# Moving a weight-staging loop's transfers from SyncE's queue to ScalarE's, with fetches two steps ahead

## The chip, the core and the metric

The kernel runs on one core of one Trainium2 chip. The metric is the device time of one execution in microseconds (us). Before the change the median of three runs is 2617.11 us (2611.94 to 2621.6). The profiled execution, from which all durations below come, took 2616.91 us.

## What is computed

One inference step of a decoder trunk with two layers on 1024 prompt tokens and 8 x 8 sample tokens, 1088 in all, with 1024 channels, in float32. Every layer adds three things to the running state h:

```python
def swiglu_ffn(x, w_gu, w_down):
    g, u = jnp.split(x @ w_gu, 2, axis=-1)
    return (jax.nn.silu(g) * u) @ w_down
...
        h = h + mix
        h = h + swiglu_ffn(rms_norm(h, g_ffn[i]), ffn_w_gu[i], ffn_w_down[i])
        gate = jax.nn.sigmoid(rms_norm(h, g_ple[i]) @ ple_w_gate[i])
        h = h + gate * (p[i] @ ple_w_proj[i])
```

The mixer `mix` is a short gated convolution in layer 0 and a Conformer convolution module in layer 1. A final norm follows. The states of the convolutions are outputs too.

## The kernel before

**Products.** Every weight matrix is cut into units of 128 x 1024 float32 (512 KB); the array `wall` holds them in the order of first use. A float32 product is made from three float32r products: `block` multiplies the weight's rounded part `whi` with both parts of the activation and the weight's remainder `wlo` with the first. A unit has 8 blocks of 128 x 128. With all 1088 tokens (three chunks of 288, 512 and 288 columns) a block is 9 matmuls.

**Preparing a unit.** `fetch_to` (L175) fetches a raw unit from SyncE's queue into one of two buffers `wraw`. `prep_to` rounds it on ScalarE (`whi`) and subtracts on GpSimd (`wlo` = `wraw` - `whi`). There are three buffers each of `whi` and `wlo`, so that a unit is prepared when TensorE has finished the unit three earlier. Right after the subtraction's place in the program the next raw unit is fetched; that fetch waits until GpSimd has read the old one.

**Staging.** From the end of layer 0's mixer on, most units are used twice, since the 1088 tokens are then split into two groups (GA, GB). While layer 0's feed-forward runs (`ffn(GJ, 0, ...)`, all 1088 tokens at once), `stage` computes the remainders of the 110 later units ahead of time and stores them in DRAM (`dlo`); `prep_to` then fetches a staged remainder (L221) where it would else subtract. `item` calls `stage` after every block, and it acts when TensorE's modelled time has moved on by STAGE_EVERY = 6.3. One step does three things:

- it stores the remainder of the step before (`dlo` <- `slo`, L242, SyncE's queue);
- it fetches a raw unit (`sraw` <- `wall`, L247, SyncE's queue; two buffers);
- it rounds the unit fetched in the step before (`shi`, ScalarE, one buffer) and subtracts (`slo` = `sraw` - `shi`, GpSimd, three buffers).

What is left when the layer's last product has been emitted is staged at once, in a loop in `run`.

**The feed-forward layer.** 22 tiles of 128 hidden channels. For each, `up` makes two items of 8 blocks, one unit each: the gate, then the other half. Behind the gate's item come VectorE (`t` = ps x r), ScalarE (silu, `t` <- `t`) and GpSimd (`t` x r); behind the second item come VectorE (`t` = ps x `t`), ScalarE (`act`, the rounded part) and VectorE (`act`'s remainder). After each group of hidden tiles (FFN_SPLIT = [3, 2, 2, 3, 3, 3, 3, 3]) `hidden` emits one more up tile and then eight down items of 3 or 2 blocks, each with a VectorE add into h (`add_h`: `h` <- `ps`, `h`), which frees the item's PSUM tile. In this stretch there are two PSUM tiles `ps`.

**Order.** Nothing is scheduled by a tool: every engine and every queue carries out its instructions in the order in which the program emits them. A helper (`Paced`, L121) stands between, so that all compute instructions have the line L121 in the profile; the tiles' names tell them apart. DMAs have their own lines.

Of the kernel before, what the change touches and what calls it, by code (L numbers as in the profile page):

```python
# [13 lines left out]
F32 = mybir.dt.float32  # L14
F32R = mybir.dt.float32r
AF = mybir.ActivationFunctionType
ALU = mybir.AluOpType
PSUM = bass.MemoryType.PSUM

P = 128  # L20
D = 1024
KD = D // P
# [115 lines left out]
class Net:  # L138
# [92 lines left out]
    def stage(self):  # L231


        nc = self.nc
        if nc.tensor.at < self.stage_at or self.pst is None:
            return
        self.stage_at = max(self.stage_at + self.STAGE_EVERY, nc.tensor.at - 2 * self.STAGE_EVERY)
        done, self.staging = self.staging, None
        if done is not None:
            u, lo = done  # L240
            self.staged[u] = self.pd.tile([P, KD * P], F32, name=f"dlo{u}")
            nc.sync.dma_start(self.staged[u], lo.bitcast(F32))  # L242
        ready = list(self.stage_raw)
        if self.to_stage:
            u = self.to_stage.popleft()
            raw = self.pst.tile([P, KD * P], F32, name="sraw", tag="sraw", bufs=2)
            nc.sync.dma_start(raw, self.wall[u])  # L247
            self.stage_raw.append((u, raw))
        if ready:
            u, raw = self.stage_raw.popleft()  # L250
            hi, lo = (
                self.pst.tile([P, KD * P], F32R, name=n, tag=n, bufs=b) for n, b in (("shi", 1), ("slo", 3)))
            nc.scalar.wait(nc.tensor)
            nc.scalar.activation(hi, raw, AF.Copy)
            nc.gpsimd.wait(nc.scalar)
            nc.gpsimd.tensor_tensor(lo, raw, hi.bitcast(F32), ALU.subtract)
            self.staging = u, lo


    def block(self, g, ps, blk, x, first, last):  # L260
# [619 lines left out]
    def run(self):  # L880
# [44 lines left out]
        for j in range(KD):  # L925
# [3 lines left out]
            if j == 5:  # L929
                self.prep_to(self.RING)  # L930
            if j >= self.LAG:
                self.norm_stat(GJ, j - self.LAG, nc.vector)
        for j in range(KD - self.LAG, KD):
            self.norm_stat(GJ, j, nc.vector)
# [122 lines left out]
    T_BUFS = 5  # L1057
    COST_B = 1.6
    STAGE_EVERY = 6.3
    LAG = 3  # L1060
    WARM = 12
    RB_GATE = 4
# [119 lines left out]
```

## Time and profile before

| | |
|---|---|
| median of three runs | 2617.11 us |
| profiled execution | 2616.91 us, of it the span 2615.1 us |
| TensorE busy | 2538.8 us (97%) |
| weight loads (PEld) busy | 2300.0 us (88%) |
| VectorE, ScalarE, GpSimd busy | 1091.9 (42%), 911.2 (35%), 992.9 us (38%) |
| mean granted TensorE clock | 0.986 |
| DMA queue of SyncE (q1) | 424.53 MB, 47.8% of 16 engines' span |
| DMA queue of ScalarE (q10) | 2.23 MB, 0.3% |

PE is TensorE, PEld its weight loads, DVE VectorE, ACT ScalarE, POOL GpSimd, SPq and ACTq the issuing of DMAs on SyncE and ScalarE. "Idle before, releaser" names what ended an engine's idle time. A DMA's issue is short; "to landing" is the time from the issue until the data are there. DMA-issuing instructions do not count as busy time of their engine.

### The profile page before, as it was taken

The numbers are of one execution on the slowest core, as the hardware profiler recorded it, in microseconds if no ns is written. First come the engines' busy times: TensorE is split into PE (matmuls) and PEld (weight loads), VectorE is DVE, ScalarE is ACT, GpSimd is POOL, SyncE is SP. The second block draws the span as 40 slices with busy tenths as digits, with TensorE's granted clock in tenths as the row PEclk, the third lists the DMA queues.
The fourth block names the chain that finished last, engine by engine and source line by source line (L and its number), as shares of the span: only waits on it lengthen the run. The fifth ranks groups of instructions, "written<-read, shape, count | busy, mean of one in ns | idle before, by whom it ended". The sixth has DMA issues, their size and how long they took to land.

```text
span 2615.1 us, 36216 instructions
## 1 busy us (share of the span) xinstructions
PE 2538.8 (97%) x15062; PEld 2300.0 (88%) x15062; DVE 1091.9 (42%) x1546; ACT 911.2 (35%) x1106; POOL 992.9 (38%) x552
## 2 busy tenths in 40 slices
PE   9999999899899999989999999999999999999997
PEld 8999998798798898989879997888887899999997
DVE  5222242222212212123487776788875442222235
ACT  5111133232222222223554545444335532222235
POOL 3323245665565665655233333333332210000012
PEclk9999999999999999999999999999999999999999
DMA  3111113555555555554555465555555575444445
GB/s 129 58 50 43 42 49 134 179 186 185 185 176 195 182 175 189 180 195 143 174 195 191 173 175 185 186 187 189 187 192 180 198 258 199 168 165 166 162 163 196
DMA packets 143236, 429.07 MB, mean 164 GB/s; under 512 B 33888, under 2 KB 37344, under 8 KB 143072
## 3 DMA queue, kind: packets, MB, share of 16 engines
q1 hardware_dynamic: 141920, 424.53, 47.8%
q8 instruction: 118, 1.93, 0.3%
q10 hardware_dynamic: 1152, 2.23, 0.3%
q14 instruction: 46, 0.38, 0.0%
HBM read 358.94 MB, written 67.76 MB: 163 GB/s over the span
## 4 chain that ended last, share of the span: by engine, by line
PE 53%; DVE 2%; ACT 1%; DMA 1%; issue 0%; POOL 0%; DVEq 0%; SPq 0%; ACTq 0%
PE ps L121 53%; DVE t L121 0%; DMA wlo<-dlo 0%; DVE h L121 0%; DVE acc L121 0%; DMA dlo<-slo 0%; DVE act L121 0%; DVE hna L121 0%; DVE nt L121 0%; ACT ua L121 0%; ACT act L121 0%; ACT cact L121 0%; DVE nv L121 0%; POOL slo L121 0%; ACT whi L121 0%
## 5 line engine op out<-in xcount | busy, mean ns | idle before, releaser
L121 PE MATMUL ps<-hn,whi 128*128 128x288 f32 (+3 forms) x6528 | 1324.9, 325 | 2.6 <-ACT whi L121 2.4
L121 PEld LDWEIGHTS ps<-hn,whi 128*128 128x128 f32 x6528 | 1014.2, 189 | 88.3 <-ACT whi L121 2.6
L121 PE MATMUL ps<-hn,wlo 128*128 128x288 f32 (+3 forms) x3264 | 796.3, 325 | 3.2 <-DMA wlo<-dlo 3.2
L121 PE MATMUL ps<-act,whi 128*128 128x288 f32 (+1 forms) x2496 | 526.0, 336 | 48.3 <-DVE h L121 44.0
L121 PEld LDWEIGHTS ps<-hn,wlo 128*128 128x128 f32 x3264 | 525.3, 189 | 45.3 <-DMA wlo<-dlo 3.4
L121 PEld LDWEIGHTS ps<-act,whi 128*128 128x128 f32 x2496 | 398.0, 193 | 90.8 <-DVE h L121 46.4
L121 ACT ACTIVATE whi<-wraw 128x1024 fp32r<-128x1024 f32 (+1 forms) x326 | 339.1, 1042 | 275.6 <-PE ps L121 238.3
L121 POOL TENSOR_TENSOR slo<-sraw,shi 128x1024 fp32r<-128x1024 f32 x110 | 263.7, 2398 | 306.0 <-ACT shi L121 256.4
L121 POOL TENSOR_TENSOR t<-t,r 128x1088 f32<-128x1088 f32 (+2 forms) x74 | 136.3, 1842 | 544.3 <-ACT t L121 499.2
L121 POOL TENSOR_TENSOR wlo<-wraw,whi 128x1024 fp32r<-128x1024 f32 (+1 forms) x98 | 258.7, 2641 | 159.4 <-ACT whi L121 143.3
L121 DVE TENSOR_TENSOR h<-ps,h 128x1088 f32<-128x1088 f32 (+2 forms) x216 | 205.0, 952 | 249.8 <-PE ps L121 249.5
L121 PE MATMUL ps<-act,wlo 128*128 128x288 f32 (+1 forms) x1248 | 309.1, 334 | 0.0
L121 ACT ACTIVATE shi<-sraw 128x1024 fp32r<-128x1024 f32 x110 | 116.6, 1060 | 520.1 <-DMA sraw<-wall 487.9
L121 DVE TENSOR_TENSOR t<-ps,t 128x1088 f32<-128x1088 f32 (+2 forms) x89 | 80.8, 908 | 425.4 <-PE ps L121 330.7
L121 DVE TENSOR_TENSOR t<-ps,r 128x512 f32<-128x512 f32 (+4 forms) x138 | 107.4, 780 | 309.8 <-PE ps L121 309.0
L121 POOL TENSOR_TENSOR sqacc<-sqacc,sq 128x512 f32<-128x512 f32 (+4 forms) x76 | 117.9, 1552 | 275.1 <-ACT sq L121 274.7
L121 PEld LDWEIGHTS ps<-act,wlo 128*128 128x128 f32 x1248 | 203.1, 192 | 19.1
L121 POOL TENSOR_TENSOR prod<-prod 128x512 f32<-128x512 f32 x96 | 124.3, 1303 | 182.8 <-ACT prod L121 182.7
L121 DVE TENSOR_TENSOR act<-t,act 128x1088 fp32r<-128x1088 f32 (+2 forms) x74 | 98.8, 1336 | 169.3 <-ACT act L121 169.3
L121 ACT ACTIVATE t<-t 128x512 f32<-128x512 f32 (+4 forms) x106 | 75.8, 716 | 244.9 <-DVE t L121 244.8
L121 ACT ACTIVATE act<-t 128x1088 fp32r<-128x1088 f32 (+2 forms) x74 | 62.1, 839 | 250.0 <-DVE t L121 250.0
L121 DVE SCALAR_TENSOR_TENSOR acc<-ub,vecs_sb,acc 128x512 f32<-128x512 f32 x184 | 137.7, 750 | 4.0 <-ACT acc L121 4.0
(123 smaller groups left out, 1684.5 us busy)
## 6 DMA issues: line engine op xcount, KB each, us to landing
wraw<-wall SPq DMA_DIRECT2D x322, 512.0 KB, 3.9
wlo<-dlo SPq DMA_DIRECT2D x226, 512.0 KB, 3.4
sraw<-wall SPq DMA_DIRECT2D x110, 512.0 KB, 6.7
dlo<-slo SPq DMA_DIRECT2D x110, 512.0 KB, 5.4
h<-xT SPq DMA_DIRECT2D x8, 544.0 KB, 6.9
pp<-t SPq DMA_DIRECT2D x8, 288.0 KB, 2.4
ub<-pp SPq DMA_DIRECT2D x8, 288.0 KB, 4.8
pp<-t SPq DMA_DIRECT2D x8, 256.0 KB, 2.7
```

What stands on the lines that cost most here:

```text
L121: return f(out, *args, **kw)
```

## The change

Staging's stores and raw fetches are issued from ScalarE. The fetch runs two steps ahead of its use (STAGE_AHEAD), with five buffers `sraw`. GpSimd writes the remainder over the raw unit, so that `slo` is gone; `dlo` is stored from `sraw`. In one step the order is now: store of the step before, rounding, subtraction, fetch. The memory is the same (six tiles of 128 x 1024 in both). The planner's model of ScalarE's time is brought up to TensorE's at each step; the order on TensorE and VectorE is the same as before.

```diff
         done, self.staging = self.staging, None
+        nc.scalar.wait(nc.tensor)
         if done is not None:
             u, lo = done
             self.staged[u] = self.pd.tile([P, KD * P], F32, name=f"dlo{u}")
-            nc.sync.dma_start(self.staged[u], lo.bitcast(F32))
-        ready = list(self.stage_raw)
+            nc.scalar.dma_start(self.staged[u], lo)
+        ready = len(self.stage_raw) == self.STAGE_AHEAD or not self.to_stage
+        if ready and self.stage_raw:
+            u, raw = self.stage_raw.popleft()
+            hi = self.pst.tile([P, KD * P], F32R, name="shi", tag="shi", bufs=1)
+            nc.scalar.activation(hi, raw, AF.Copy)
+            nc.gpsimd.wait(nc.scalar)
+            nc.gpsimd.tensor_tensor(raw.bitcast(F32R), raw, hi.bitcast(F32), ALU.subtract)
+            self.staging = u, raw
         if self.to_stage:
             u = self.to_stage.popleft()
-            raw = self.pst.tile([P, KD * P], F32, name="sraw", tag="sraw", bufs=2)
-            nc.sync.dma_start(raw, self.wall[u])
+            raw = self.pst.tile([P, KD * P], F32, name="sraw", tag="sraw", bufs=self.STAGE_AHEAD + 3)
+            nc.scalar.dma_start(raw, self.wall[u])
             self.stage_raw.append((u, raw))
-        if ready:
-            u, raw = self.stage_raw.popleft()
-            hi, lo = (
-                self.pst.tile([P, KD * P], F32R, name=n, tag=n, bufs=b) for n, b in (("shi", 1), ("slo", 3)))
-            nc.scalar.wait(nc.tensor)
-            nc.scalar.activation(hi, raw, AF.Copy)
-            nc.gpsimd.wait(nc.scalar)
-            nc.gpsimd.tensor_tensor(lo, raw, hi.bitcast(F32), ALU.subtract)
-            self.staging = u, lo
...
     STAGE_EVERY = 6.3
+    STAGE_AHEAD = 2
```

ScalarE's queue early in the layer, from one up tile's silu (`t<-t`) over its second unit to its `act` and into the next unit. Before:

```order
L121 ACTIVATE t<-t 128x1088
L121 ACTIVATE whi<-wraw 128x1024
L121 ACTIVATE shi<-sraw 128x1024 x2
L121 ACTIVATE act<-t 128x1088
L121 ACTIVATE whi<-wraw 128x1024
```

The same place after the change:

```order
L121 ACTIVATE t<-t 128x1088
L121 ACTIVATE whi<-wraw 128x1024
L121 DMA dlo_3355<-sraw 128x1024
L121 ACTIVATE shi<-sraw 128x1024
L121 DMA sraw<-wall 128x1024
L121 DMA dlo_3398<-sraw 128x1024
L121 ACTIVATE shi<-sraw 128x1024
L121 DMA sraw<-wall 128x1024
L121 ACTIVATE act<-t 128x1088
L121 ACTIVATE whi<-wraw 128x1024
```

Each rounding now stands between a store and a fetch; two of each lie ahead of `act`. SyncE's queue at about the same place (`dlo` with a number is one staged unit in DRAM). Before:

```order
L175 DMA wraw<-wall 128x1024
L242 DMA dlo_3258<-slo 128x1024
L247 DMA sraw<-wall 128x1024
L242 DMA dlo_3302<-slo 128x1024
L247 DMA sraw<-wall 128x1024
L175 DMA wraw<-wall 128x1024
```

After, from the mixer's last state outputs to the first remainders fetched back:

```order
L476 DMA sa_p<-u_2458 128x2
L477 DMA sa_s<-u_2458 1024x1x2
L175 DMA wraw<-wall 128x1024 x68
L221 DMA wlo<-dlo_3183 128x1024
L175 DMA wraw<-wall 128x1024
L221 DMA wlo<-dlo_3250 128x1024
L175 DMA wraw<-wall 128x1024
```

The staged fetches and stores that stood between weight fetches are gone from this queue: 68 weight fetches follow one another. At the layer's start ScalarE has, before, `whi`, `shi`, `whi`, `sh` (the norm's sum), and after the change `whi`, `whi`, `sh`, `shi`, since the first rounding comes one step later.

## Prediction

> **What bounds the kernel now.** I read the page's totals first, then what TensorE waited for, then the stretch in which staging runs. The page's first lines and the list of TensorE's waits (us in total, times, longest):
>
> ```profile
> span 2615.1 us, 36216 instructions
> PE 2538.8 (97%) x15062; PEld 2300.0 (88%) x15062; DVE 1091.9 (42%) x1546; ACT 911.2 (35%) x1106; POOL 992.9 (38%) x552
> ...
> PE ps L121 <- DVE h L121: 44.0, 7, 10.3
> ...
> PE st L121 <- DVE sl L121: 1.3, 1, 1.3
> ```
>
> TensorE is busy for 97% of the span, so only its holes and its slow stretches can be won. 44.0 us of some 76 us of holes are seven waits for a VectorE add into h. Next, busy time by stretches (us: PE busy with its matmuls, the other engines, granted clock, DMA share, GB/s): a clean stretch, a staging stretch, and the whole first feed-forward layer. Behind them comes its costliest waiting group:
>
> ```profile
> 100.00:200.00 100.00, 100.00 (x605) 91.12 (x604) 23.87 (x24) 14.98 (x16) 28.99 (x16) 1.00 0.15 46
> 600.00:700.00 100.00, 87.85 (x506) 79.78 (x507) 27.48 (x21) 25.07 (x25) 56.98 (x23) 0.93 0.51 174
> 393.60:1253.40 859.80, 810.79 (x4761) 735.08 (x4760) 214.20 (x153) 248.35 (x247) 508.75 (x204) 0.97 0.52 176
> ```
> ```profile
> L121 PE MATMUL ps<-act,whi 128*128 128x288 f32 (+1 forms) x1056 | 217.8, 344 | 47.2 <-DVE h L121 44.0 <-DVE t L121 2.7 <-DVE act L121 0.5
> ```
>
> The clean stretch runs 605 matmuls in 100 us, 165.3 ns each. At that pace the layer's 4761 need 787.0 us; it takes 859.8. So 72.8 us are lost in it. All seven waits for h lie in it, with 2.7 for t, 0.5 for act and 1.3 for the norm's sum: 48.5 us stand still, and the other 24 us are matmuls at a lower clock behind those stops (0.93 granted in 600 to 700).
>
> What makes h late? The timeline around one of the seven, engine by engine (start, duration, what, [idle before <- releaser]):
>
> ```profile
> 1009.20 0.33 SPq L175 DMA_DIRECT2D wraw<-wall  x1
> 1009.58 0.42 SPq L242 DMA_DIRECT2D dlo<-slo  x1
> 1010.05 0.43 SPq L247 DMA_DIRECT2D sraw<-wall  x1
> ```
> ```profile
> 1016.56 1.06 ACT L121 ACTIVATE shi<-sraw 128x1024 fp32r<-128x1024 f32 x1 [11.15 <-DMA sraw<-wall]
> 1017.52 1.09 ACT L121 ACTIVATE act<-t 128x1088 fp32r<-128x1088 f32 x1
> ```
> ```profile
> 1007.53 1.29 DVE L121 TENSOR_TENSOR t<-ps,t 128x1088 f32<-128x1088 f32 x1 [10.70 <-PE ps L121]
> 1018.65 2.54 DVE L121 TENSOR_TENSOR act<-t,act 128x1088 fp32r<-128x1088 f32 x1 [9.82 <-ACT act L121]
> 1021.11 2.48 DVE L121 TENSOR_TENSOR h<-ps,h 128x1088 f32<-128x1088 f32 x2
> ```
> ```profile
> 1006.75 2.42 POOL L121 TENSOR_TENSOR wlo<-wraw,whi 128x1024 fp32r<-128x1024 f32 x1
> ```
> ```profile
> 1022.44 1.94 PE L121 MATMUL ps<-act,whi 128*128 128x288 f32 x5 [6.14 <-DVE h L121]
> ```
>
> VectorE has t at 1008.8. ScalarE could make act then, but shi stands ahead of it in its queue and waits for a staged tile until 1016.56. So act comes 8.7 us late, h behind it, and TensorE, with both PSUM tiles full, stops for 6.14. The tile was asked for only at 1010.05: SyncE was held at the weight fetch (L175) until GpSimd finished wlo at 1009.17, and the staged fetch queues behind that. The totals for 400 to 1215 say that this is the rule (ScalarE, then SyncE):
>
> ```profile
> ACT shi L121 <- DMA sraw<-wall: 487.9, 63, 12.5
> ACT shi L121 <- POOL slo L121: 32.0, 39, 1.6
> ```
> ```profile
> SPq L175 <- POOL wlo L121: 626.3, 63, 16.4
> ```
>
> It is a ring of latencies: shi, GpSimd's subtractions, SyncE, a landing, the next shi.
>
> **The change part by part.** Its durations (min/median/max ns, first and last start us; landings in us) for sraw, for slo, and for the eight DMAs that ScalarE issues today:
>
> ```profile
> L247 SPq DMA_DIRECT2D sraw<-wall x110: 328/430/778, 403.1 to 1204.8; - x110
> L121 ACT ACTIVATE shi<-sraw x110: 1041/1061/1067, 407.6 to 1210.6; 128x1024 fp32r<-128x1024 f32 x110
> DMA to landing us min/median/max: 4.5/6.7/9.0
> ```
> ```profile
> L121 POOL TENSOR_TENSOR slo<-sraw,shi x110: 2343/2402/2441, 408.7 to 1212.3; 128x1024 fp32r<-128x1024 f32 x110
> L242 SPq DMA_DIRECT2D dlo<-slo x110: 326/423/1481, 414.9 to 1214.7; - x110
> DMA to landing us min/median/max: 3.6/5.4/8.4
> ```
> ```profile
> L121 ACTq DMA_DIRECT2D praw<-pT x8: 334/358/454, 1260.0 to 1468.6; - x8
> ```
>
> *Fetch two steps ahead.* The 110 fetches spread over 801.7 us, 7.36 us a step; without the layer's loss of 72.8 a step is (801.7 - 72.8)/109 = 6.7 us. A tile asked for two steps ahead has 13.4 us to land, against 9.0 at worst. ScalarE's 487.9 us at shi go, and with them the lateness of act. SyncE keeps only weight fetches in this stretch: 626.3 us of waiting stay there, with nothing staged behind.
>
> *Store on ScalarE.* It waits for GpSimd's subtraction of the step before. Queued behind it: shi, the next fetch, act, whi. But shi waits for the same subtraction today, since its one buffer is read by it (the 32.0 us row); the wait moves one place ahead and costs nothing new. The fetch gains a wait: its buffer, one of five, is free once the store issued two steps earlier has landed, 8.4 at worst against 13.4. Nothing there either.
>
> *220 issues on ScalarE.* One costs 0.33 (praw's minimum) to 1.48 us (the worst store on SyncE); I take 0.43, sraw's median, some 95 us in all, which leaves ScalarE well under half used. What matters is the place ahead of act, so I lay out the last up unit, with these rows besides:
>
> ```profile
> L121 DVE TENSOR_TENSOR t<-ps,r x22: 1278/1292/1293, 420.6 to 1204.9; 128x1088 f32<-128x1088 f32 x22
> L121 ACT ACTIVATE t<-t x22: 1091/1113/1117, 424.4 to 1206.3; 128x1088 f32<-128x1088 f32 x22
> L121 POOL TENSOR_TENSOR t<-t,r x22: 2498/2540/2572, 425.6 to 1207.5; 128x1088 f32<-128x1088 f32 x22
> ```
> ```profile
> L121 POOL TENSOR_TENSOR wlo<-wraw,whi x64: 2361/2408/3467, 400.3 to 1220.4; 128x1024 fp32r<-128x1024 f32 x64
> L121 ACT ACTIVATE whi<-wraw x63: 1039/1043/1066, 408.5 to 1219.3; 128x1024 fp32r<-128x1024 f32 x63
> ```
> ```profile
> L121 DVE TENSOR_TENSOR act<-t,act x22: 1293/2600/3381, 430.6 to 1219.4; 128x1088 fp32r<-128x1088 f32 x22
> ```
>
> Let TensorE end that unit at 0; it began at 72 x 165.3 ns before, at -11.9. VectorE's t: -10.6. Silu: -9.5. whi, store, shi, fetch: -6.5. GpSimd from -9.5: t, wlo, first subtraction: -2.1. Then the second store, shi and fetch on ScalarE: -0.2. VectorE's t of the second half comes at 1.3, so act starts on time with 1.5 us in hand. At 1.48 per issue the last fetch ends near 1.9, 0.6 late.
>
> From there: t 1.3, act 2.4, VectorE's act 3.7 to 5.0 (1.29 free, 2.60 beside GpSimd), h 5.0 to 6.3. TensorE needs that PSUM tile after two down items: two times three blocks of 9 matmuls, 8.9 us, or in the two groups with two blocks, 6.0 us. Slack 2.6 in the former; up to 0.3 missing in the latter. I keep 0.5 at each of those two, the 0.5 for act at the layer's end, and 1.5 for small stops: 3 us.
>
> *Remainder over the raw tile.* The same 110 subtractions; only the destination is new. No row shows one in place at this size, but t<-t,r is in place: 2.54 us for 1088 columns, 2.33 ns a column, against 2.34 for slo. The bound is the slowed 3.47 of wlo's row: +1.07 each, covered by GpSimd's idle time (508.75 busy of 859.8).
>
> *Order at the start.* With the first shi behind sh, the norm's sum no longer waits for a staged tile: the 1.3 goes with the rest.
>
> Sum, against the profiled execution's own time of 2616.9 (span 2615.1 and 1.8 around it; the median of the three timed runs is 2617.1, the same): 2616.9 - 72.8 + 3 = 2547. The clean pace is uncertain by one matmul in 605, 1.3 us on 787; I say 2548.
>
> How much of the loss comes back with the stops hangs on the clock. Behind the 2.7 us stop at 501 (start, duration) six matmuls took 2.02 us, and 1.17 a little later:
>
> ```profile
> 503.36 2.02 PE L121 MATMUL ps<-act,whi 128*128 128x288 f32 x6
> ...
> 506.08 1.17 PE L121 MATMUL ps<-act,whi 128*128 128x288 f32 x6
> ```
>
> So even this stop, short beside the others, has slow matmuls behind it, and I let all 24 us go. The Trainium skill ("TensorE: Matmul & The Clock Gate", "HAM oscillation") has half rate only behind idle gaps over about 3.4 us, one window of that length each. By that rule five or six of the stops would cost 1.7 us each, the gain would be 48.5 + 10 - 3, and the time, as an estimate from that page, 2561. The trace disagrees: it misses 24 us where the rule has 10.
>
> **The rivals.** *ScalarE or GpSimd is late next (2556 to 2595).* Issues at 1.48 make act 0.6 late, felt only at the two short groups; subtractions at 3.47 make the last up unit's GpSimd work 2.5 + 3 x 3.5 = 13 us against 11.9. Then some of the seven stops stay at a few us each, each with its slow matmuls (24 lost beside 48.5: half as much again). Half of the loss kept is 2616.9 - 36 = 2581. For it: GpSimd is the busiest helper here (56.98 of 100). Against: it now idles, waiting for shi.
>
> *No change (2604 to 2630).* If staged tiles asked for by ScalarE landed later than 13.4 us, shi would wait as now. Against: the DMA share is 0.52 over the layer, and the tile above landed 6.5 us after its issue; the delay was ahead of the issue. The Trainium skill ("DMA: Bandwidth & Descriptors", "Issuing engines are not separate DMA queues") speaks for this rival: issuing from several engines saves only the sequencer's issue time. The trace shows what that leaves out here: 626.3 us of waiting ahead of the issues.
>
> *Slower (2640 and up).* The fetch now holds ScalarE until the store of two steps earlier has landed. With landing L, two steps take L + 2 us (issues and shi). Against 13.4 this begins at L = 11.4; at L = 12.7 the 55 pairs take 55 x 14.7 = 809 against 737, as much as today's loss, and at 14 they take 880, so 2616.9 - 72.8 + 143 = 2687. It needs landings 1.5 times the worst seen, from two queues colliding. Against: the rows show 8.4 at worst, with weight fetch, store and staged fetch issued within a microsecond as above; the change spreads them.
>
> **How the numbers follow.** Forecast 0.76, late helpers 0.12, no change 0.06, slower 0.06. What a measurement can tell from no change is about 0.5%, 13 us, so faster is 0.76 + 0.12 = 0.88, within 0.06, slower 0.06. The range begins at 2538. The fastest clean stretch of the trace is this:
>
> ```profile
> 200.00:300.00 100.00, 100.00 (x608) 91.40 (x607) 23.96 (x24) 16.04 (x17) 30.77 (x17) 1.00 0.14 44
> ```
>
> At its 164.5 ns the layer's loss is 76.7; with nothing kept that is 2540, and 2 us are for the spread of runs. The range ends at 2580, which takes in the better half of the late helpers.
>
> **What would show it.** In the changed profile: TensorE's wait for h in 400 to 1215 falls from 44.0 to a few us; ScalarE's wait for sraw nearly vanishes, and some of it reappears at the stores as a wait for GpSimd; the layer takes about 790 us at a clock near 1.00; sraw's landing stays under 13 us. A wait of act's group for ScalarE with issues over 1 us would show the first rival; waits of ScalarE's own fetches for stores, the last; shi still waiting for landings, the second. I am wrong if the layer still takes over 825 us.

## The result and the profile after

The changed kernel takes 2546.8 us in the median of four runs (2546.1 to 2547.9), the kernel before 2616.5, also of four (2611.9 to 2621.6): a ratio of 0.9733, 95% interval 0.9715 to 0.9752. 2548 was forecast, within 2538 to 2580. The profiled execution took 2547.9 us.

First the page of the changed kernel, then its list of TensorE's waits in 400 to 1215 (us in total, times, longest):

```profile
span 2546.1 us, 36304 instructions
PE 2518.0 (99%) x15062; PEld 2283.9 (90%) x15062; DVE 1068.5 (42%) x1546; ACT 909.6 (36%) x1106; POOL 978.0 (38%) x552
```
```profile
PE ps L121 <- DVE t L121: 1.7, 1, 1.7
PE ps L121 <- DVE act L121: 0.5, 1, 0.5
```

The row with seven waits for h, 44.0 us, is gone; two stops are left in the stretch, 2.2 us together. By stretches, the same clean one, the same staging one, and the whole layer:

```profile
100.00:200.00 100.00, 100.00 (x603) 90.94 (x603) 23.87 (x24) 14.98 (x16) 29.00 (x16) 1.00 0.16 48
600.00:700.00 100.00, 100.00 (x607) 91.35 (x606) 22.80 (x18) 29.64 (x30) 60.26 (x25) 1.00 0.56 193
393.60:1183.00 789.40, 787.12 (x4760) 717.97 (x4759) 190.65 (x152) 247.22 (x248) 493.68 (x204) 1.00 0.56 192
```

The staging stretch now runs 607 matmuls in 100 us where it ran 506, as many as the clean one (603). The layer takes 789.4 us instead of 859.8: 70.4 us less, and the two profiled executions lie 69.0 apart: all of the gain is in this layer. The granted clock is 1.00 instead of 0.97, so the slow matmuls went with the stops.

The same place in the program as the one shown of before, the end of the last up unit of the same group, on ScalarE, VectorE and TensorE:

```profile
956.17 0.33 ACTq L121 DMA_DIRECT2D dlo<-sraw  x1
956.61 1.06 ACT L121 ACTIVATE shi<-sraw 128x1024 fp32r<-128x1024 f32 x1 [5.91 <-POOL sraw L121]
956.69 0.34 ACTq L121 DMA_DIRECT2D sraw<-wall  x1
959.68 1.11 ACT L121 ACTIVATE act<-t 128x1088 fp32r<-128x1088 f32 x1 [2.02 <-DVE t L121]
```
```profile
958.35 1.29 DVE L121 TENSOR_TENSOR t<-ps,t 128x1088 f32<-128x1088 f32 x1 [10.70 <-PE ps L121]
960.83 1.29 DVE L121 TENSOR_TENSOR act<-t,act 128x1088 fp32r<-128x1088 f32 x1 [1.18 <-ACT act L121]
962.72 1.29 DVE L121 TENSOR_TENSOR h<-ps,h 128x1088 f32<-128x1088 f32 x1 [0.60 <-PE ps L121]
```
```profile
958.08 1.15 PE L121 MATMUL ps<-act,whi 128*128 128x288 f32 x6
```

TensorE ends the unit at 958.08. The second rounding runs before that, and ScalarE then stands idle for 2.02 us until VectorE has t: act now waits for its input, no longer for a staged tile. h waits for TensorE, not TensorE for h.

The waits of ScalarE at shi and of SyncE in 400 to 1215, and the staged fetch's row:

```profile
ACT shi L121 <- POOL sraw L121: 242.0, 54, 6.2
```
```profile
SPq L175 <- POOL wlo L121: 737.6, 64, 22.5
```
```profile
L121 ACTq DMA_DIRECT2D sraw<-wall x110: 334/358/1752, 396.9 to 1127.1; - x110
```

The 487.9 us of waiting for sraw are gone from ScalarE. Its wait for GpSimd's subtraction grew from 32.0 to 242.0: ScalarE now arrives early and waits there instead, and no wait of TensorE comes of it. SyncE waits longer than before (737.6 against 626.3), with nothing staged behind.

### The profile page after: what moved, and what is told of

Its sections match the earlier page's. It is cut to its first block, busy times and chain, and to the rows that moved or that the text cites. A ratio compares the mean times of both kernels' runs of the same rounds, so it can differ in the third digit from the quotient of the medians.

```text
span 2546.1 us, 36304 instructions
## 1 busy us (share of the span) xinstructions
PE 2518.0 (99%) x15062; PEld 2283.9 (90%) x15062; DVE 1068.5 (42%) x1546; ACT 909.6 (36%) x1106; POOL 978.0 (38%) x552
## 4 chain that ended last, share of the span: by engine, by line
PE 96%; DVE 2%; ACT 1%; DMA 0%; issue 0%; DVEq 0%; SPq 0%; ACTq 0%
PE ps L121 96%; DVE t L121 0%; DVE nt L121 0%; DMA wlo<-dlo 0%; DVE acc L121 0%; DVE h L121 0%; DVE hna L121 0%; DVE nv L121 0%; DVE act L121 0%; DMA h<-xT 0%; ACT ua L121 0%; ACT act L121 0%; ACT L121 0%; ACT cact L121 0%; DVE r L121 0%
## 5 line engine op out<-in xcount | busy, mean ns | idle before, releaser
L121 PE MATMUL ps<-act,whi 128*128 128x288 f32 (+1 forms) x2496 | 511.8, 329 | 1.5 <-DVE act L121 1.4
L121 PEld LDWEIGHTS ps<-act,whi 128*128 128x128 f32 x2496 | 387.4, 188 | 39.8 <-DVE act L121 2.6
L121 POOL TENSOR_TENSOR wlo<-wraw,whi 128x1024 fp32r<-128x1024 f32 (+1 forms) x98 | 240.6, 2457 | 249.7 <-ACT whi L121 233.4
L121 PE MATMUL ps<-act,wlo 128*128 128x288 f32 (+1 forms) x1248 | 303.3, 328 | 0.0
L121 POOL TENSOR_TENSOR sraw<-sraw,shi 128x1024 fp32r<-128x1024 f32 x110 | 265.7, 2415 | 79.9 <-issue 61.3
L121 ACT ACTIVATE shi<-sraw 128x1024 fp32r<-128x1024 f32 x110 | 115.7, 1052 | 242.8 <-POOL sraw L121 242.0
L121 DVE SCALAR_TENSOR_TENSOR acc<-ua,vecs_sb,acc 128x512 f32<-128x512 f32 x184 | 129.2, 750 | 6.3 <-ACT acc L121 4.8
```

The lines of the kernel that those rows point to most:

```text
L121: return f(out, *args, **kw)
```

## The experiments

The change does three things at once that could each bring the tile in time or relieve GpSimd: another queue, a longer lead, other buffers. Three theories stood against each other. A: a staged tile that comes late holds ScalarE at shi, and act with it; whatever brings the tile in time gives the whole gain. B: the gain is one of buffers (`slo` gone). C: the gain needs the second queue. The first four kernels take the change apart. Each ratio is to runs of the kernel before that were timed along with the experiment; their medians lie between 2616.5 and 2619.6, so two or three microseconds between kernels of different series say nothing.

**Only the buffers are left: both transfers on SyncE, one step ahead.** The edit against the changed kernel:

```diff
-            nc.scalar.dma_start(self.staged[u], lo)
+            nc.sync.dma_start(self.staged[u], lo)
...
-            nc.scalar.dma_start(raw, self.wall[u])
+            nc.sync.dma_start(raw, self.wall[u])
...
-    STAGE_AHEAD = 2
+    STAGE_AHEAD = 1
```

> The changed kernel with both transfers back on SyncE and one step of lead; what is left of the change is the remainder written over the raw tile (no slo, four buffers of sraw). Theory A (a late staged tile holds ScalarE at shi, and act with it): the hold on SyncE and the lead are as before, so the time stays near 2617, 2605 to 2625, with waits for h of 40 us or so. Theory B (the gain is one of buffers: GpSimd no longer waits for a free slo): most of the 70 us come back, 2550 to 2570.

Measured: 2616.1 us against 2617.2 of before, ratio 0.9999 (0.9989 to 1.0009). TensorE's and ScalarE's waits in its layer:

```profile
PE ps L121 <- DVE h L121: 43.2, 7, 10.0
```
```profile
ACT shi L121 <- DMA sraw<-wall: 486.0, 65, 11.7
```

Both rows are within 2 us of those of before (44.0 and 487.9). The remainder written over the raw tile brings nothing and costs nothing. Theory B falls.

**Only the lead: both transfers on SyncE, two steps ahead.** The same edit without its last two lines.

> The changed kernel with both transfers back on SyncE; the lead of two steps stays. Theory A: a staged fetch is still held behind the weight fetch, by up to a whole GpSimd subtraction, but it is asked for about 12 us earlier, which covers hold and landing together (some 7 + 7 us against 14.5): waits at shi for sraw fall under 60 us in all, and the time is 2547 to 2556. Theory C (what counts is the second queue: transfers no longer line up behind one another): the gain is lost, 2595 to 2620.

Measured: 2547.6 us (2546.1 to 2550.8), ratio 0.9736 (0.9722 to 0.9751). The waits of ScalarE and SyncE, and the landing of the staged fetch (median us, last number):

```profile
ACT shi L121 <- DMA sraw<-wall: 19.4, 14, 2.9
```
```profile
SPq L175 <- POOL wlo L121: 567.4, 63, 18.7
```
```profile
sraw<-wall SPq DMA_DIRECT2D x110, 512.0 KB, 7.0
```

SyncE is held almost as long as before (567.4 us against 626.3), and a tile takes 7.0 us to land, no less than the 6.7 of before. Asked for one step earlier, it comes in time all the same. Theory C falls.

**Only the queue: ScalarE, one step ahead.** STAGE_AHEAD = 1 in the changed kernel.

> The changed kernel with one step of lead instead of two, still from ScalarE. Theory A: without SyncE's hold a tile is asked for 5 to 7 us before its use and lands in about 4, so shi waits 0 to 3 us a step, act is up to 2 us late, and only the two short groups stop: 2550 to 2565. If the lead alone made the gain: back to 2600 and more. Theory C: as the changed kernel, 2547.

Measured: 2549.1 us (2548.6 to 2553.5), ratio 0.9744 (0.9729 to 0.9758): better than theory A's 2550 to 2565. shi waits little for landings:

```profile
ACT shi L121 <- DMA sraw<-wall: 14.8, 13, 4.4
```

None of it reaches TensorE, whose waits in the layer are the 1.7 and 0.5 us of the changed kernel.

**None of the change: the hold on SyncE taken away.** The edit against the kernel before; while staging runs, the weight fetch goes out one unit later, when GpSimd has as a rule long read its buffer:

```diff
-            self.fetch_to(u + 1 + self.RAW + len(self.spare))
+            self.fetch_to(u + self.RAW + len(self.spare) + (self.pst is None))
```

> The kernel before with one edit outside staging: while staging runs, the weight fetch is emitted one unit later, when its buffer has long been free, so that SyncE is not held there. Staging is as before: SyncE's queue, one step of lead, slo. Theory A: the hold is the cause, so most of the gain comes without any of the change: waits at shi of 0 to 3 us a step, 2550 to 2575. Theory C (a second queue is needed) and theory B (slo's buffers): no gain, 2605 to 2625.

Measured: 2548.2 us (2546.6 to 2549.9), ratio 0.9737 (0.9722 to 0.9751). SyncE's waits and ScalarE's at shi:

```profile
SPq L242 <- POOL slo L121: 551.8, 110, 16.4
SPq L175 <- POOL wlo L121: 58.1, 15, 12.2
```
```profile
ACT shi L121 <- DMA sraw<-wall: 23.5, 17, 4.0
```

The wait ahead of the weight fetch falls to 58.1 us, and with one line outside staging the whole gain is there, on one queue, with one step of lead. SyncE still waits some 600 us: most of it now stands ahead of a store, for staging's own subtraction of the step before, and a staged fetch that goes out behind that still lands in time for its use one step later. So it is not the length of the queue's waiting that costs, but that the fetch needed next stood behind a wait for something else. Theory A holds, in a stronger form than expected: the queue, the lead and the removed hold each give the whole gain, as far as these runs can tell them apart (2549.1, 2547.6, 2548.2).

The next four put a price on the two rivals that the prediction feared.

**A fetch that waits for the store of its own step.** Three buffers in place of five (`bufs=self.STAGE_AHEAD + 1`).

> The changed kernel with three buffers of sraw instead of five: the fetch at the end of a step waits for the store issued at the head of the same step. This is the mechanism of the slower rival, a fetch that holds ScalarE, at the landing time that the chip has (2.9 us in the median). Hand-laid: store, shi 1.06, then about 1.5 to 2 us of holding a step; in the last up unit the second fetch ends near 1.6 instead of -0.2, so act is 0.3 us late. Theory A: 2547 to 2553, no loss beyond the two short groups. If any hold on ScalarE reaches TensorE: 14 steps ahead of the seven down groups at 2 us and slow matmuls behind them, 2560 to 2580.

Measured: 2547.8 us (2545.5 to 2548.5), ratio 0.9733 (0.9718 to 0.9747), no wait for h. ScalarE has that time to spare.

**The same hold ahead of the rounding.** Three buffers, and the fetch, which waits for the store, moved in front of shi:

```diff
             nc.scalar.dma_start(self.staged[u], lo)
         ready = len(self.stage_raw) == self.STAGE_AHEAD or not self.to_stage
+        if self.to_stage:
+            u = self.to_stage.popleft()
+            raw = self.pst.tile([P, KD * P], F32, name="sraw", tag="sraw", bufs=self.STAGE_AHEAD + 1)
+            nc.scalar.dma_start(raw, self.wall[u])
+            self.stage_raw.append((u, raw))
         if ready and self.stage_raw:
```

> The changed kernel with three buffers and the fetch moved ahead of the rounding, directly behind the store that it waits for: now the whole landing of each store (2.9 us) holds ScalarE and GpSimd's subtraction with it, in all 110 steps. This is the slower rival's mechanism at its full size. Hand-laid: in the last up unit act comes some 2.2 us late, inside the 2.6 us of slack of the groups of three, outside that of the two groups of two: stops near 2.5 us there, each with about 2 us of slow matmuls behind, 2552 to 2562. If a hold of ScalarE goes to TensorE step by step (110 x 2.9): 2700 and more.

Measured: 2578.2 us (2569.0 to 2581.7), ratio 0.9838 (0.9817 to 0.9858): a loss of some 31 us against the changed kernel, where 5 to 15 had been worked out. ScalarE's queue through two steps, and TensorE's wait:

```profile
974.38 0.33 ACTq L121 DMA_DIRECT2D dlo<-sraw  x1
977.02 0.33 ACTq L121 DMA_DIRECT2D sraw<-wall  x1
977.46 1.06 ACT L121 ACTIVATE shi<-sraw 128x1024 fp32r<-128x1024 f32 x1 [3.69 <-DMA dlo<-sraw]
981.62 0.33 ACTq L121 DMA_DIRECT2D dlo<-sraw  x1
984.25 0.33 ACTq L121 DMA_DIRECT2D sraw<-wall  x1
984.69 1.06 ACT L121 ACTIVATE shi<-sraw 128x1024 fp32r<-128x1024 f32 x1 [6.17 <-DMA dlo<-sraw]
985.65 1.10 ACT L121 ACTIVATE act<-t 128x1088 fp32r<-128x1088 f32 x1
...
988.31 0.33 ACTq L121 DMA_DIRECT2D dlo<-sraw  x1
```
```profile
PE ps L121 <- DVE h L121: 23.2, 7, 6.6
```

The expectation laid out one unit from a clean start. But store, landing, fetch, rounding and subtraction now form a ring: two steps take 988.31 - 974.38 = 13.9 us, while TensorE needs 72 x 165.3 ns = 11.9 us for the unit in which they lie. ScalarE falls behind over units that hold two steps, makes some of it up where a unit holds one, and all seven groups stop again. From the first store to the last a step takes (1183.2 - 414.5)/109 = 7.05 us, in the changed kernel (1150.5 - 413.7)/109 = 6.76. It is the old disease at half strength, with another member in the ring.

**More work on ScalarE.** Each rounding done three times, and twice:

```diff
-            nc.scalar.activation(hi, raw, AF.Copy)
+            for _ in range(3):
+                nc.scalar.activation(hi, raw, AF.Copy)
```

The twofold kernel has `range(2)`.

> The changed kernel with each rounding shi done three times over (the same values again): 2.1 us more of ScalarE in each step, ahead of GpSimd's subtraction, which starts that much later. It measures the margin that ScalarE has ahead of act, laid out as 1.5 us, with 2.6 us of slack behind it in the groups of three. Theory A: act 1 to 3 us late in the last up unit; stops of 1 to 3 us in the two short groups and up to 1 us in the others, with slow matmuls behind: 2549 to 2562. If ScalarE has no margin (every addition reaches TensorE at the seven groups, two steps each): 7 x 4.2 plus half as much again, some 2590.

> The changed kernel with each rounding shi done twice (the same values again): 1.06 us more of ScalarE in each step, half of what the threefold rounding added (that took 2557). By the hand-laid last up unit the margin ahead of act is 1.5 us; the second fetch ends near 0.9 instead of -0.2, and act can start at 1.3, on time. So: 2546 to 2550, no new stop for h. If the loss grows evenly with ScalarE's work instead of beginning at a margin, half of the threefold's: 2552.

Measured: threefold 2557.4 us (2555.5 to 2561.8), ratio 0.9777 (0.9760 to 0.9793); twofold 2546.8 (2544.3 to 2547.8), ratio 0.9721 (0.9705 to 0.9738). The first 1.06 us a step are free, the second cost 10.6 us: the loss begins at a margin between them, and the 1.5 us of the hand-laid unit fit, though two points do not fix it. The ring fits as well, and takes in the kernel with the hold first: where only its own work holds it up, a step takes 947.77 - 942.62 = 5.2 us from store to store in the twofold kernel, 954.79 - 948.54 = 6.2 in the threefold and 988.31 - 981.62 = 6.7 with the hold first. Two of them are 10.3, 12.5 and 13.4 us against the unit's 11.9, and the losses are none, 10.6 and 31 us. In the threefold kernel TensorE waits for h three times, 4.2 us in all, and 1.9 for act.

No run beat the changed kernel by more than its spread; the one-line kernel and the changed one tie.

## Why the prediction was right, point by point

- **The sum.** 72.8 lost, 3 kept: the layer was to come to 790.0, it came to 789.4. That the remainder fits so well is luck, for it is not what I had kept. The two groups of two blocks do not stop at all: VectorE's act took 1.29 us there, not 2.60, since GpSimd no longer subtracts at that moment. Its row, before 1293/2600/3381 ns, is now:

```profile
L121 DVE TENSOR_TENSOR act<-t,act x22: 1291/1292/2047, 429.6 to 1151.1; 128x1088 fp32r<-128x1088 f32 x22
```

- **The lead.** A fetch goes out 13.4 us ahead of its rounding in the median, as laid out. But the steps come unevenly, and the shortest lead is 8.8 us (fetch at 586.66, rounding at 595.42), less than the worst landing of before (9.0). It was enough because landings fell to 5.9 us at worst, which the prediction did not forecast.

- **The norm at the start** was wrong in its size. The 1.3 for the sum went as forecast, but 1.7 came back ten microseconds later, as TensorE's wait for t. One of the steps ahead of t on VectorE ran beside a staged subtraction:

```profile
415.99 3.37 DVE L121 SCALAR_TENSOR_TENSOR nt<-nt,nv 128x1088 f32<-128x1088 f32 x1
419.40 1.29 DVE L121 SCALAR_TENSOR_TENSOR r<-nt,r 128x1088 f32<-128x1088 f32 x1
```

  Two like operations on 1088 columns, 3.37 and 1.29 us. The subtraction beside the first, and the same operation in the threefold kernel, where the next subtraction starts only at 416.62:

```profile
415.66 2.56 POOL L121 TENSOR_TENSOR sraw<-sraw,shi 128x1024 fp32r<-128x1024 f32 x1 [1.99 <-ACT shi L121]
```
```profile
414.42 1.29 DVE L121 SCALAR_TENSOR_TENSOR nt<-nt,nv 128x1088 f32<-128x1088 f32 x1
```

  In that kernel TensorE does not wait for t. So the overlap is the cause. The Trainium skill ("SBUF — State Buffer", "Who interferes with whom") has VectorE and GpSimd take turns at a shared port; the rows agree with that.

- **The store's wait for GpSimd** costs nothing, as forecast. That some of the wait for sraw would reappear there was forecast too, but not that it would be 242.0 us: the length of a wait on a helper says little by itself.

- **The issues on ScalarE.** Priced at 0.43 each and all of them in line. In the median they take 0.33 (stores) and 0.36 (fetches), and they need not stand in line: the fetch at 956.69 goes out while the rounding begun at 956.61 still runs. ScalarE stands idle for 2.02 us ahead of that act, where 1.5 had been laid out.

- **The clock.** That all 24 us come back with the stops was right. The 2561 worked out from the Trainium skill ("TensorE: Matmul & The Clock Gate", "HAM oscillation") lies outside all four runs. TensorE behind a long stop in the kernel before, then behind a middling and a short one in the threefold kernel, then behind a stop of 2.69 us in the kernel with the hold first and one of 1.72 in the changed kernel:

```profile
685.45 2.18 PE L121 MATMUL ps<-act,whi 128*128 128x288 f32 x6 [10.31 <-DVE h L121]
...
690.77 0.52 PE L121 MATMUL ps<-act,whi 128*128 128x288 f32 x2
```
```profile
656.77 1.61 PE L121 MATMUL ps<-act,whi 128*128 128x288 f32 x6 [2.75 <-DVE h L121]
...
659.08 1.99 PE L121 MATMUL ps<-act,whi 128*128 128x288 f32 x6
...
661.40 1.15 PE L121 MATMUL ps<-act,whi 128*128 128x288 f32 x6
```
```profile
500.31 1.26 PE L121 MATMUL ps<-act,whi 128*128 128x288 f32 x6 [0.93 <-DVE h L121]
```
```profile
881.05 1.28 PE L121 MATMUL ps<-act,whi 128*128 128x288 f32 x6 [2.69 <-DVE h L121]
...
884.19 1.18 PE L121 MATMUL ps<-act,whi 128*128 128x288 f32 x6
```
```profile
422.16 1.25 PE L121 MATMUL ps<-hn,whi 128*128 128x288 f32 x6 [1.72 <-DVE t L121]
...
425.24 1.16 PE L121 MATMUL ps<-hn,whi 128*128 128x288 f32 x6
```

  Behind 10.31 us of standing still the next two blocks took 690.77 - 685.45 = 5.3 us instead of 3.0; behind 2.75 us they took 661.40 - 656.77 = 4.6 us instead of 3.0. So 1.6 us are lost behind a stop of 2.75. That is shorter than the gap of about 3.4 us from which the Trainium skill ("TensorE: Matmul & The Clock Gate", "HAM oscillation") warns of half rate. But behind 2.69 the two blocks took 884.19 - 881.05 = 3.1 us, and behind 1.72 they took 425.24 - 422.16 = 3.1, next to nothing lost; behind 0.93 it is the same. Between 1 and 3.5 us a stop's length alone does not decide, and what does stays open.

- **The cause, and what of the change did it.** The chain from SyncE's hold to h was right, and the experiments show it from three sides. What the prediction did not see is that the change does more than is needed: it takes the queue and the lead together, and never asks whether one alone would do; either would have.

- **The rivals.** The first, a late ScalarE or GpSimd, was not met: no wait for h is left. The kernel with the hold first shows what it looks like: ScalarE late, by a ring that is too long. The second, no change, named the right doubt for the wrong reason. The Trainium skill ("DMA: Bandwidth & Descriptors", "Issuing engines are not separate DMA queues") says that another issuing engine saves only the time of the issue. That fits here insofar as a second queue is not needed: SyncE alone gives 2547.6. What a change of queue can bring is that a transfer no longer stands behind another's wait. The third, slower, was not met: it needed landings over 11 us, and they are 2.9 (stores) and 4.1 (fetches) in the median, 5.9 at worst. A relative of it exists: with the hold ahead of the rounding one such landing a step costs 31 us.

## What to carry to other kernels

In these traces an engine issues its transfers in the order of the program: a prefetch that stands behind a transfer which waits for a buffer goes out no earlier than that buffer is free. Before moving it to another queue, see whether the waiting transfer can go out later, when its buffer is free: one line here. To judge a helper's lateness, add up the ring that feeds it (issue, landing, work, release) and hold it against the time of the engine that sets the pace, over the units that hold most steps; laying out a single unit from a clean start misses a ring that is only a little too long.

## What the runs showed of the hardware

The same 512 KB fetch lands in 4.1 us in the median from ScalarE's queue, 6.7 before and 7.0 in the kernel with only the lead from SyncE's queue, where it goes out within a microsecond or two of a weight fetch and a store; the store lands in 2.9 and 5.4. With SyncE alone and the hold gone it lands in 5.0. It did not matter for the time. A stop of TensorE can cost more than its length, but the surcharge does not grow with it: behind the seven waits for h in the kernel before (3.31 to 10.31 us) the next two blocks lost 1.6 to 2.6 us, 2.6 behind 4.84 and 2.3 behind 10.31. Behind 2.75 it was 1.6, and behind 1.72 and 2.69 some 0.1 to 0.2; even a stop of 3.43 us, in the kernel with only the buffers left, cost no more.
